# Seven half-block products for eight in the first product of the last MLP

## The chip, the cores and the metric

The kernel runs on one core of a Trainium2 chip. The metric is the device time of one execution in microseconds (us), lower is better; times given are the median of several executions. Engines are named as in the profile: PE is the matrix engine (TensorE), PEld its weight loads, DVE the vector engine, ACT the scalar engine, POOL GpSimd, SP the engine whose queue issues most of the transfers.

## The reference, cut to what matters

The network has two layers over 1024 tokens of width 1024. Each layer is a mixer and then an MLP with a squared ReLU of inner width 4096; a norm ends it. The change touches the MLP of the second layer.

```python
def sqrelu_mlp(h, w1, w2):
    return jnp.square(jax.nn.relu(h @ w1)) @ w2

def reference(x, ...):
    for layer in range(DEPTH):
        ...
        x = x + mix.astype(x.dtype)
        h = rmsnorm(x, norm_ffn_g[layer])
        x = x + sqrelu_mlp(h, mlp_w1[layer], mlp_w2[layer]).astype(x.dtype)
    return rmsnorm(x, final_norm_g)
```

## The kernel before, in words

The tokens are worked on as two halves of 512 (H). Activations lie transposed: 8 chunks (NK) of 128 features by 512 tokens. A product in float32 is made from three matmuls in the faster type fp32r: every operand is split into a rounded part and a rest, and `mm3` (L304 to L310) multiplies rounded weight by rounded input (L308), rounded weight by the input's rest (L309) and the weight's rest by the rounded input (L310). Each matmul has a weight tile of 128 by 128 and streams 512 columns.

`weights` (L275 to L300) brings weights in pieces of 256 KB: SP issues the transfer into `wraw` (L286), ACT casts it to `whi` (L291), and the rest `wlo` is a subtraction in `lo` (L266 to L272), two of three times on DVE and otherwise on POOL. `wraw`, `whi` and `wlo` are rings of 4 slots: a slot is written again when its last reader is done.

`mlp` (L1204) takes the inner width in 8 blocks of 4 tiles of 128 features (f-tiles). `first(fb, fts)` makes one f-tile after another: 8 chunks by 3 matmuls into one PSUM tile `mm` (a ring of 6), then ReLU and square on ACT (L1225, L1226), a cast to `hidh` (L1232) and the rest `hidl` (L272). `second(fb)` multiplies the block by its rows of the second weight matrix, 4 output pieces of 24 matmuls with two PSUM tiles each, and DVE adds each to the residual `x` (L1253). With `ahead` = 2, two f-tiles of block b+1 come before the second product of block b and two behind it. Both products of a block have 96 matmuls of 512 columns.

At the end of the program the last MLP runs first for the last block (7) of half 0, whose residual is `x0`. Then `final(0, x0)` (L1374) writes half 0's rows: for each of four groups u of 128 tokens it makes 4 transposes into the PSUM tile `lnn` and 4 into `lnl` (L1384), ACT squares and sums both (L1372), DVE adds the two sums (L1365), ACT takes a root (L1366), DVE a reciprocal (L1367) and two scaled copies into `fo` (L1390), and SP issues the transfer out (L1393). There is one `lnn` and one `lnl`, so the transposes of u+1 into a tile wait until DVE has copied u out of it. Then comes the last MLP for half 1, all 8 blocks, whose last block is closed by `final_rows` (L1397). A scheduler lays out each engine's order from the program, so that f-tiles of half 1's block 0 stand among the transposes of `final(0)`; within `second` and `first` PE's order is the order written.

Of the kernel before, what the change touches and what calls it, by code (L numbers as in the profile page):

```python
# [9 lines left out]
F32 = mybir.dt.float32  # L10
F32R = mybir.dt.float32r
AF = mybir.ActivationFunctionType
ALU = mybir.AluOpType
# [4 lines left out]
P = 128  # L18
D = 1024
S = 1024  # L20
H = 512
NK = D // P
# [23 lines left out]
class Net:  # L46
# [258 lines left out]
    def mm3(self, ps, whi, wlo, xhi, xlo, start, stop):  # L305
        mm = self.nc.tensor.matmul
        self.clk += 0.64
        mm(ps, lhsT=whi, rhs=xhi, start=start, stop=False)  # L308
        mm(ps, lhsT=whi, rhs=xlo, start=False, stop=False)  # L309
        return mm(ps, lhsT=wlo, rhs=xhi, start=False, stop=stop)  # L310

    def mmps(self):
        return self.mm.tile([P, H], F32, "mm")
# [191 lines left out]
    def norm0(self):  # L505
# [3 lines left out]
        self.r0 = yield from self.rstd(accs, self.eps[:, 0:1], self.tp)  # L509
        self.done.add("r0")  # L510

    def scaled(self, xs, r, gname, w):
        nc = self.nc
        his, los = self.hpair(w)
# [686 lines left out]
        return xs  # L1201


    def mlp(self, layer, halves, blocks, ahead, dve=None, close=None, keep=None, beside=None):  # L1204
# [7 lines left out]
        hids = {}  # L1212

        def first(fb, fts):
            hid = hids.setdefault(fb, [([], []) for _ in halves])
            for ft in fts:
                f = fb * 4 + ft
                whi, wlo = self.weight(w1[:, :, f * P:(f + 1) * P], NK, P, dve, (1, f), keep)
                for hh, (xs, (his, los)) in zip(hid, halves):
                    ps = self.mmps()  # L1220
                    for k in range(NK):
                        mm = self.mm3(ps, whi[k], wlo[k], his[k], los[k], k == 0, k == NK - 1)
                        yield 0
                    t = self.tp.tile([P, H], F32, name="rel", tag="rel")
                    nc.scalar.activation(out=t, in_=ps, func=AF.Relu)  # L1225
                    nc.scalar.activation(out=t, in_=t, func=AF.Square)  # L1226
                    hi = self.hid.tile([P, H], F32R, "hidh")
                    lo = self.hid.tile([P, H], F32R, "hidl")
                    if dve is False:
                        nc.scalar.copy(out=hi, in_=t)  # L1230
                    else:
                        nc.vector.tensor_copy(out=hi, in_=t)  # L1232
                    last = self.lo(lo, t, hi, True if beside else dve)
                    hh[0].append(hi)
                    hh[1].append(lo)
                    if beside:
                        beside(last, mm)

        def second(fb):
            hid = hids.pop(fb)  # L1240
            for oc in range(4):
                whi, wlo = self.weight(w2[:, fb * 4:fb * 4 + 4, oc * 256:(oc + 1) * 256], 4, 256, dve, (2, fb, oc), keep)
                for hh, (xs, _) in zip(hid, halves):
                    pss = [self.mmps() for _ in range(2)]
                    for ks in (range(3), range(3, 4)):
                        for o in range(2):
                            for k in ks:
                                mm = self.mm3(pss[o], whi[k][:, o * P:(o + 1) * P], wlo[k][:, o * P:(o + 1) * P], hh[0][k],
                                         hh[1][k], k == 0, k == 3)
                                yield 0  # L1250
                    for o in range(2):
                        x = xs[oc * 2 + o]
                        last = nc.vector.tensor_tensor(out=x, in0=pss[o], in1=x, op=ALU.add)  # L1253
                    if beside:
                        beside(last, mm)

        blocks = list(blocks)
        yield from first(blocks[0], range(4))
        for i, fb in enumerate(blocks):
            if i + 1 < len(blocks):  # L1260
                yield from first(blocks[i + 1], range(ahead))
            if close and i + 1 == len(blocks):
                (his, los), = hids.pop(fb)
# [185 lines left out]
    def run(self):  # L1449
        nc = self.nc  # L1450
# [6 lines left out]
        _, mp = self.pool("mm", bufs=1, space=PSUM)  # L1457
# [39 lines left out]
        def main():  # L1497
            yield from self.cols0(h0)
            h1 = yield from self.cols1()
            self.close(cmst)  # L1500
            yield "b"
            self.mm.slots = mmslots + [(self.sp, "sc1", 2)] * 2
            _, hidp = self.pool("hid", side="left")
            self.hslots = [(hidp, f"hid{i}") for i in range(8)]
            self.hid = Ring(self.hslots)
            _, self.tp = self.pool("tmp", bufs=3, side="left")
            self.nt, self.ntp = "rel", self.tp
            _, xp = self.pool("x0", side="left")
# [57 lines left out]
        self.conv_out(c1, x1)  # L1566
        n1 = self.norm(x1, "nf1", 1)
        self.go(self.mlp(1, [(x0, n0)], [7], 0))
        _, self.fp = self.pool("fin", bufs=1, side="right")
        gp = self.gfin = self.fp.tile([P, D], F32, name="gfin")  # L1570
        nc.scalar.dma_start(out=gp, in_=self.A["final_norm_g"].rearrange("(o d) -> o d", o=1).to_broadcast([P, D]))
        self.final(0, x0)
        self.go(self.mlp(1, [(x1, n1)], range(8), 2, close=lambda *a: self.final_rows(1, x1, *a)))
        while self.open:
            self.close()

# [28 lines left out]
```

## Time and profile before

| | |
|---|---|
| time, median of 3 executions | 2381.07 us (2380.44 to 2381.91) |
| profiled execution, its own time | 2379.74 us |
| its span | 2378.0 us |
| PE busy | 2308.1 us, 97% of the span |
| DVE, ACT, POOL busy | 1532.2, 1047.7, 542.8 us |
| mean granted PE clock (1 is full) | 0.992 |

Durations come from the profiled execution, which is 1.33 us under the median. The page's busy column counts a matmul from its start to the end that the profile models, and matmuls overlap; the pace of a stream of matmuls is read from the distance of their starts. "idle before <-" is idle time of the engine just before an instruction, and what ended it.

### The profile page before, as it was taken

How to read it: one execution, taken by the hardware profiler on the slowest of the kernel's cores; microseconds unless marked ns; L12 is line 12 of the kernel's file. 1: busy time of each engine (PE TensorE's matmuls, PEld its weight loads, DVE VectorE, ACT ScalarE, POOL GpSimd, SP SyncE). 2: the span in 40 equal slices, each digit the busy share in tenths (PEclk: the TensorE clock that was granted, in tenths of full speed). 3: DMA queues.
4: the chain of work that ended last, by engine and by line, in shares of the span. 5: the costliest groups of instructions: out<-in, count | busy, mean ns of one | idle time of the engine just before them, and what ended most of it. 6: DMA issues, size and time to landing. Idle time of an engine off the chain costs nothing.

```text
span 2378.0 us, 38508 instructions
## 1 busy us (share of the span) xinstructions
PE 2308.1 (97%) x14535; PEld 1856.4 (78%) x14535; DVE 1532.2 (64%) x2563; ACT 1047.7 (44%) x1874; POOL 542.8 (23%) x477
## 2 busy tenths in 40 slices
PE   8989889989999999999999999999999999999998
PEld 6767667767777787878888888888878778888887
DVE  7775743667555464569977653799999756533334
ACT  6546634556443332443443363534433544433333
POOL 2322433110111121322000000105555422221121
PEclk9999999999999999999999999999999999999999
DMA  7345234444445454546666665563323333433332
GB/s 219 111 110 153 83 88 132 109 127 123 136 143 178 126 175 133 169 133 200 198 195 191 194 183 172 144 188 98 98 89 98 99 93 94 129 95 98 98 97 85
DMA packets 417934, 320.12 MB, mean 135 GB/s; under 512 B 44642, under 2 KB 360276, under 8 KB 417748
## 3 DMA queue, kind: packets, MB, share of 16 engines
q1 hardware_dynamic: 413684, 309.79, 43.5%
q0 software_dynamic: 2176, 4.19, 0.6%
q10 hardware_dynamic: 1888, 3.67, 0.5%
q8 instruction: 114, 1.87, 0.3%
q14 instruction: 72, 0.59, 0.1%
HBM read 257.29 MB, written 60.29 MB: 134 GB/s over the span
## 4 chain that ended last, share of the span: by engine, by line
PE 75%; DVE 15%; DMA 4%; ACT 3%; issue 2%; SPq 0%; POOL 0%; DVEq 0%; ACTq 0%; POOLq 0%
PE mm L308 23%; PE mm L309 22%; PE mm L310 22%; DVE acc L1321 5%; DMA raw<-p 1%; PE sc L734 1%; DVE C L709 1%; DVE E L711 1%; PE sc L652 1%; DVE hidl L272 1%; PE sc L817 1%; PE sc L771 1%; DMA cx<-d 1%; DVE x L1253 1%; PE at L936 1%
## 5 line engine op out<-in xcount | busy, mean ns | idle before, releaser
L291 ACT CAST whi<-wraw 128x512 fp32r<-128x512 f32 x720 | 445.7, 621 | 986.9 <-PE mm L309 890.9
L308 PE MATMUL mm<-h,whi 128*128 128x512 f32 x1792 | 725.8, 406 | 7.1 <-ACT h L383 2.4
L310 PE MATMUL mm<-h,wlo 128*128 128x512 f32 x1792 | 704.1, 394 | 1.4 <-POOL wlo L272 1.4
L309 PE MATMUL mm<-h,whi 128*128 128x512 f32 x1792 | 703.3, 393 | 1.3 <-DVE h L272 1.0
L272 POOL TENSOR_TENSOR wlo<-wraw,whi 128x512 fp32r<-128x512 f32 x302 | 422.2, 1399 | 1233.8 <-ACT whi L291 1178.5
L1321 DVE SCALAR_TENSOR_TENSOR acc<-u,par,acc 128x512 f32<-128x512 f32 x480 | 429.8, 905 | 10.0
L308 PEld LDWEIGHTS mm<-h,whi 128*128 128x128 f32 x1792 | 339.7, 190 | 89.7 <-issue 12.8
L310 PEld LDWEIGHTS mm<-h,wlo 128*128 128x128 f32 x1792 | 339.1, 189 | 75.7 <-POOL wlo L272 2.3
L309 PEld LDWEIGHTS mm<-h,whi 128*128 128x128 f32 x1792 | 340.0, 190 | 69.0 <-issue 2.4
L308 PE MATMUL mm<-hidh,whi 128*128 128x512 f32 x992 | 389.4, 396 | 0.1
L309 PE MATMUL mm<-hidl,whi 128*128 128x512 f32 x992 | 386.0, 390 | 0.9 <-DVE hidl L272 0.9
L310 PE MATMUL mm<-hidh,wlo 128*128 128x512 f32 x992 | 384.5, 390 | 0.9 <-POOL wlo L272 0.9
L272 DVE TENSOR_TENSOR wlo<-wraw,whi 128x512 fp32r<-128x512 f32 x258 | 183.5, 712 | 200.9 <-ACT whi L291 193.2
L1253 DVE TENSOR_TENSOR x<-mm,x 128x512 f32<-128x512 f32 x248 | 166.5, 686 | 85.9 <-PE mm L310 85.5
L308 PEld LDWEIGHTS mm<-hidh,whi 128*128 128x128 f32 x992 | 186.2, 188 | 43.5 <-issue 4.2
L310 PEld LDWEIGHTS mm<-hidh,wlo 128*128 128x128 f32 x992 | 186.2, 188 | 40.3 <-POOL wlo L272 1.3
L309 PEld LDWEIGHTS mm<-hidl,whi 128*128 128x128 f32 x992 | 186.3, 188 | 40.0 <-DVE hidl L272 1.3
L272 DVE TENSOR_TENSOR hidl<-rel,hidh 128x512 fp32r<-128x512 f32 x109 | 84.9, 780 | 77.9 <-ACT hidh L1230 76.5
L1232 DVE CAST hidh<-rel 128x512 fp32r<-128x512 f32 x68 | 34.2, 506 | 89.8 <-ACT rel L1226 89.6
L1226 ACT ACTIVATE rel<-rel 128x512 f32<-128x512 f32 x128 | 80.6, 633 | 3.9 <-ACT rel L1225 0.4
L1225 ACT ACTIVATE rel<-mm 128x512 f32<-128x512 f32 x128 | 75.6, 593 | 2.2 <-DVE hidl L272 2.0
L1557 POOL COPY u<-u 128x30 f32<-128x30 f32 x8 | 3.2, 399 | 250.2 <-DVE acc L1321 250.2
(377 smaller groups left out, 2191.9 us busy)
## 6 DMA issues: line engine op xcount, KB each, us to landing
wraw<-in_mlp_w_dram SPq DMA_DIRECT2D x512, 256.0 KB
lo<-wlo SPq DMA_DIRECT2D x160, 256.0 KB
wlo<-lo SPq DMA_DIRECT2D x160, 256.0 KB
wraw<-in_cv_pw_w_dram SPq DMA_DIRECT2D x96, 256.0 KB
wraw<-in_hy_w_in_dram SPq DMA_DIRECT2D x80, 256.0 KB
wraw<-in_hy_w_out_dram SPq DMA_DIRECT2D x32, 256.0 KB
p<-stg SPq DMA_DIRECT2D x30, 256.0 KB
raw<-p SPq DMA_DIRECT2D x40, 128.0 KB
```

Of the source, the lines that this page charges most:

```text
L272: return eng.tensor_tensor(out=out, in0=x, in1=hi.bitcast(F32), op=ALU.subtract)
L291: nc.scalar.copy(out=hi, in_=raw)
L308: mm(ps, lhsT=whi, rhs=xhi, start=start, stop=False)
L309: mm(ps, lhsT=whi, rhs=xlo, start=False, stop=False)
L310: return mm(ps, lhsT=wlo, rhs=xhi, start=False, stop=stop)
L652: mm(ps[64 * q:64 * q + 64, u * P:(u + 1) * P], lhsT=src[hs, c * 64:(c + 1) * 64], rhs=ar[hs, :, c, :], start=(u == 0), stop=(u == 3), ski ...
L709: tt(out=j3[:, 0:n, 0:m], in0=a3[:, j, j + 1:16].unsqueeze(2).to_broadcast([64, n, m]), in1=x3[:, j:j + 1, 0:m].to_broadcast([64, n, m]), ...
L1225: nc.scalar.activation(out=t, in_=ps, func=AF.Relu)
L1226: nc.scalar.activation(out=t, in_=t, func=AF.Square)
L1232: nc.vector.tensor_copy(out=hi, in_=t)
L1253: last = nc.vector.tensor_tensor(out=x, in0=pss[o], in1=x, op=ALU.add)
L1321: nc.vector.scalar_tensor_tensor(out=acc, in0=u[:, j:j + H], scalar=self.pv(f"dw{j}", c), in1=acc, op0=ALU.mult, op1=ALU.add)
```

## The change

In the last MLP of half 1 the first product of blocks 1 to 7 goes over to `first_seven`. It takes f-tiles in pairs and the 1024 input features in two halves, so that the weight is a 2 by 2 arrangement of pieces A11, A12, A21, A22 (each 256 KB, four 128 by 128 tiles). DVE makes four sums of pieces, S1 to S4, and the 2 by 2 product is made of seven products of half the input's columns (256 tokens) in place of eight: 7 pieces by 4 tiles by 3 matmuls of 256 columns for a pair, that is 168 matmuls of 256 columns for a block in place of 96 of 512. Four accumulators r1 to r4 lie by twos in two PSUM tiles; ACT copies r1 (L1282 of the changed kernel), DVE combines the accumulators (L1284 to L1294), ACT applies ReLU, square and the cast.

`half_sums` makes the matching sums of half 1's input on DVE, rounds them on ACT and takes their rests. It is written behind block 7 of half 0 and before `final(0)`. Behind `final(0)` the pool of `x0` is closed, and a pool in its space adds 2, 3 and 3 slots to the rings `wraw`, `whi`, `wlo`.

```diff
+    def half_sums(self, xs, gname, w, v):
...
+        for c in range(NK // 2):
+            ys = []
+            for k in (c, c + NK // 2):
+                y = self.ntp.tile([P, H], F32, name="nt", tag=self.nt)
+                nc.vector.scalar_tensor_tensor(out=y, in0=xs[k], scalar=self.pv(gname, k), in1=self.r, op0=ALU.mult,
+                                               op1=ALU.mult)
+                ys.append(y)
+            ta, tb = (self.tp2.tile([P, H], F32, name="lt", tag="lt") for _ in range(2))
+            tt(out=ta[:, L], in0=ys[0][:, R], in1=ys[0][:, L], op=ALU.subtract)
+            tt(out=ta[:, R], in0=ys[1][:, R], in1=ta[:, L], op=ALU.subtract)
+            tt(out=tb[:, L], in0=ys[1][:, R], in1=ys[0][:, R], op=ALU.subtract)
+            tt(out=tb[:, R], in0=ys[1][:, L], in1=ta[:, R], op=ALU.subtract)
+            for n, t in enumerate((ta, tb)):
+                nc.scalar.copy(out=h[:, 0, 2 * c + n, :], in_=t)
+                self.lo(h[:, 1, 2 * c + n, :], t, h[:, 0, 2 * c + n, :])
...
+        def first_seven(fb, pairs):
...
+            for p in pairs:
+                A = {}
+                for i in range(2):
+                    f = fb * 4 + 2 * i + p
+                    for j in range(2):
+                        a = A[f"A{i + 1}{j + 1}"] = self.wraw.tile([P, 4, P], F32, "wraw")
+                        nc.sync.dma_start(out=a, in_=w1[:, 4 * j:4 * j + 4, f * P:(f + 1) * P])
+                for name, a, b, op in (("S1", "A21", "A22", ALU.add), ("S2", "S1", "A11", ALU.subtract),
+                                       ("S3", "A11", "A21", ALU.subtract), ("S4", "A12", "S2", ALU.subtract)):
+                    A[name] = self.mip.tile([P, H], F32, name="ws", tag="mi").rearrange("p (k f) -> p k f", k=4)
+                    tt(out=A[name], in0=A[a], in1=A[b], op=op)
+                ra, rb = self.mmps(), self.mmps()
+                r1, r2, r3, r4 = ra[:, L], ra[:, R], rb[:, L], rb[:, R]
...
+                    for a, b, r, begin in (("A11", "B11", r1, True), ("S2", "T2", r2, False), ("S3", "T3", r3, True),
+                                           ("S1", "T1", r4, False), ("A12", "B21", r1, False), ("A22", "T4", r3, False),
+                                           ("S4", "B22", r4, False)):
+                        whi = self.whi.tile([P, 4, P], F32R, "whi")
+                        nc.scalar.copy(out=whi, in_=A[a])
+                        wlo = self.wlo.tile([P, 4, P], F32R, "wlo")
+                        self.lo(wlo, A[a], whi)
+                        for c in range(4):
+                            self.mm3(r, whi[:, c, :], wlo[:, c, :], *self.seven[b](c), begin and c == 0, c == 3, True)
+                            yield 0
+                        if a == "A11":
+                            nc.scalar.copy(out=u2, in_=r1)
+                        elif a == "S2":
+                            tt(out=u2, in0=r2, in1=u2, op=ALU.add)
...
+                        else:
+                            tt(out=y1[:, R], in0=r4, in1=u2, op=ALU.add)
+                for k, y, raw in ((2 + p, y2, slice(0, H)), (p, y1, R)):
+                    nc.scalar.activation(out=y[:, raw], in_=y[:, raw], func=AF.Relu)
+                    nc.scalar.activation(out=y, in_=y, func=AF.Square)
...
         self.go(self.mlp(1, [(x0, n0)], [7], 0))
+        self.half_sums(x1, "nf1", 1, 0)
...
         self.final(0, x0)
-        self.go(self.mlp(1, [(x1, n1)], range(8), 2, close=lambda *a: self.final_rows(1, x1, *a)))
+        self.close(self.cmx0)
+        _, wp3 = self.pool("w3", side="left")
+        for ring, n, m in ((self.wraw, "wraw", 2), (self.whi, "whi", 3), (self.wlo, "wlo", 3)):
+            ring.slots = ring.slots + [(wp3, f"{n}{4 + i}") for i in range(m)]
+        self.go(self.mlp(1, [(x1, n1)], range(8), 2, seven=range(1, 8), close=lambda *a: self.final_rows(1, x1, *a)))
```

How the order on the engines moves, at three places. The first is PE at the end of half 0's last second product, where `final(0)`'s transposes (into `lnn` and `lnl`, L1384 before and L1476 after) meet block 0 of half 1. Before, the rows are these, and 30 matmuls of block 0 stand between the last transposes of one token group and the first of the next:

```order
L1384 MATMUL lnn<-ident,x_4739 128x128 x3
L308 MATMUL mm<-h,whi 128x512
L309 MATMUL mm<-h,whi 128x512
L310 MATMUL mm<-h,wlo 128x512
L308 MATMUL mm<-h,whi 128x512
L309 MATMUL mm<-h,whi 128x512
L1384 MATMUL lnl<-ident,x_4739 128x128
```

After the change the first group's transposes still stand among the 24 matmuls of one f-tile, whose last three are the first rows here; the other three groups then follow each other:

```order
L308 MATMUL mm<-h,whi 128x512
L309 MATMUL mm<-h,whi 128x512
L310 MATMUL mm<-h,wlo 128x512
L1476 MATMUL lnl<-ident,x_4739 128x128 x2
L1476 MATMUL lnn<-ident,x_4739 128x128 x4
L1476 MATMUL lnl<-ident,x_4739 128x128 x4
L1476 MATMUL lnn<-ident,x_4739 128x128 x4
L1476 MATMUL lnl<-ident,x_4739 128x128 x4
L1476 MATMUL lnn<-ident,x_4739 128x128 x4
L1476 MATMUL lnl<-ident,x_4739 128x128 x4
L308 MATMUL mm<-h,whi 128x512
```

The matmuls that stood between the groups have moved behind the last group.

The second place is DVE there. After the change the last two updates of `x0` (L1345) stand among `half_sums` (L524 to L531, and the rests `h`), and the first step of `final(0)` on DVE (L1457) stands behind the last of it:

```order
L1345 TENSOR_TENSOR x_4739<-mm,x_4739 128x512
L524 SCALAR_TENSOR_TENSOR nt<-x_10850,par,acc 128x512
L1345 TENSOR_TENSOR x_4739<-mm,x_4739 128x512
L524 SCALAR_TENSOR_TENSOR nt<-x_10850,par,acc 128x512
L272 TENSOR_TENSOR h<-lt,h 128x512
L528 TENSOR_TENSOR lt<-nt 128x256
L1264 TENSOR_TENSOR ws<-wraw 128x512
L530 TENSOR_TENSOR lt<-nt 128x256
L529 TENSOR_TENSOR lt<-nt,lt 128x256
L531 TENSOR_TENSOR lt<-nt,lt 128x256
L272 TENSOR_TENSOR wlo<-wraw,whi 128x512
L272 TENSOR_TENSOR h<-lt,h 128x512
L1457 TENSOR_REDUCE fss<-fss 128x1
```

All of these but the updates and the weight's rest are new before L1457.

The third place is a block in the steady part: on PE the end of piece A11 of one pair (into `mm_21604`), two matmuls of A11 of the next pair (`mm_21759`), and then piece S2 of the first pair, which goes to the other half of `mm_21604`:

```order
L308 MATMUL mm_21604<-h_10854,whi_21611 128x256
L309 MATMUL mm_21604<-h_10854,whi_21611 128x256
L310 MATMUL mm_21604<-h_10854,wlo_21613 128x256
L308 MATMUL mm_21759<-h_10854,whi_21766 128x256 [waits DVE_49,Activation_49]
L309 MATMUL mm_21759<-h_10854,whi_21766 128x256
L308 MATMUL mm_21604<-h_78,whi_21628 128x256 [waits Activation_49]
```

On ACT the cast of that next A11 (`whi_21766`, in the slot that `whi_21611` had) stands ahead of the copy of r1 out of `mm_21604`:

```order
L1275 CAST whi_21766<-wraw_21743 128x512 [waits DMAHW3_49,PE_49]
L1282 COPY su_21608<-mm_21604 128x256 [waits PE_49]
L1275 CAST whi_21783<-ws_21753 128x512 [waits DVE_49,PE_49,Pool_49]
```

Before, the place has 48 matmuls of 512 columns in a row, each f-tile in a PSUM tile of its own.

## Rows read from the trace of the kernel before

**Rows 1.** Waits of PE from 1990 us on: total us, times, longest.
```profile
PE lnn L308 <- ACT fo L1407: 0.2, 1, 0.2
```
**Rows 2.** Busy time by stretch of the last MLP, half 1.
```profile
core 0: us, PE busy (x) PEld busy (x) DVE busy (x) ACT busy (x) POOL busy (x), PEclk, DMA share, GB/s
1990.00:2005.00 15.00, 15.00 (x68) 12.43 (x67) 13.62 (x18) 6.81 (x13) 7.06 (x5) 1.00 0.29 86
2005.00:2050.00 45.00, 45.00 (x215) 37.16 (x214) 20.33 (x36) 18.98 (x43) 8.60 (x7) 1.00 0.43 135
2094.00:2137.00 43.00, 43.00 (x191) 35.60 (x190) 16.22 (x25) 14.48 (x24) 9.02 (x7) 1.00 0.33 98
```
**Rows 3.** Timeline of PE: first matmul of 96 in one stretch, and the first behind it.
```profile
2072.27 0.39 PE L308 MATMUL mm<-h,whi 128*128 128x512 f32 x1
...
2094.03 0.39 PE L308 MATMUL mm<-hidh,whi 128*128 128x512 f32 x1
```
**Rows 4.** Timeline of PE: 256-column matmuls of the attention with 128x128 weights.
```profile
123.81 0.28 PE L896 MATMUL at<-kl,q 128*128 128x256 f32 x1
...
124.16 1.02 PE L682 MATMUL sc<-krv,blk 128*128 128x512 f32 x2
```
**Rows 5.** Timeline of PEld: the weight load of the second of these.
```profile
123.81 0.19 PEld L894 LDWEIGHTS at<-kh,q 128*128 128x128 f32 x1
```
**Rows 6.** Groups by line: durations of kinds that the change adds (mean ns).
```profile
L792 DVE TENSOR_TENSOR F<-sc,F 128x256 f32<-128x256 f32 x16 | 6.7, 419 | 13.3 <-PE sc L790 13.3
L804 ACT COPY C<-sc 128x256 f32<-128x256 f32 x16 | 5.8, 371 | 30.0 <-PE sc L803 30.0
L291 ACT CAST whi<-wraw 128x512 fp32r<-128x512 f32 x134 | 83.2, 622 | 224.3 <-PE mm L309 220.2 <-PE lnl L310 3.3 <-issue 0.8
L1226 ACT ACTIVATE rel<-rel 128x512 f32<-128x512 f32 x33 | 20.6, 634 | 0.8
L1253 DVE TENSOR_TENSOR x<-mm,x 128x512 f32<-128x512 f32 x64 | 43.5, 691 | 33.3 <-PE mm L310 33.2
```
**Rows 7.** Timeline of PE: end of half 0's last product; transposes of group 1.
```profile
2013.94 0.39 PE L310 MATMUL mm<-hidh,wlo 128*128 128x512 f32 x1
...
2025.97 0.60 PE L1384 MATMUL lnn<-ident,x 128*128 128x128 f32 x4
2026.76 0.48 PE L308 MATMUL mm<-h,whi 128*128 128x512 f32 x1
```
**Rows 8.** Timeline of ACT behind the transposes of group 1.
```profile
2026.61 0.60 ACT L1372 ACTIVATE fj<-lnn 128x512 f32<-128x512 f32 x1
```
**Rows 9.** Timeline of DVE behind the transposes of group 1.
```profile
2028.69 0.75 DVE L1390 SCALAR_TENSOR_TENSOR fo<-lnn,fss,gfin 128x512 f32<-128x512 f32 x1
2029.36 0.74 DVE L1390 SCALAR_TENSOR_TENSOR fo<-lnl,fss,gfin 128x512 f32<-128x512 f32 x1
```
**Rows 10.** Timeline of DVE where the half's input is scaled, and of block 1.
```profile
2000.90 1.77 DVE L272 TENSOR_TENSOR wlo<-wraw,whi 128x512 fp32r<-128x512 f32 x1
2003.32 1.29 DVE L1253 TENSOR_TENSOR x<-mm,x 128x512 f32<-128x512 f32 x2 [0.65 <-PE mm L310]
...
2098.06 0.69 DVE L272 TENSOR_TENSOR wlo<-wraw,whi 128x512 fp32r<-128x512 f32 x1 [1.01 <-ACT whi L291]
```
**Rows 11.** Timeline of POOL in the same places.
```profile
2000.38 1.74 POOL L272 TENSOR_TENSOR h<-nt,h 128x512 fp32r<-128x512 f32 x1
...
2108.98 1.28 POOL L272 TENSOR_TENSOR wlo<-wraw,whi 128x512 fp32r<-128x512 f32 x1 [12.94 <-ACT whi L291]
```
**Rows 12.** Timeline of PE behind an idle stretch elsewhere, in half 0.
```profile
1753.92 0.47 PE L308 MATMUL mm<-h,whi 128*128 128x512 f32 x1 [1.89 <-DVE x L1253]
...
1754.51 0.63 PE L310 MATMUL mm<-h,wlo 128*128 128x512 f32 x1
...
1757.88 0.40 PE L309 MATMUL mm<-h,whi 128*128 128x512 f32 x1
```
**Rows 13.** The stretch after that idle time, columns as in rows 2.
```profile
1754.40:1757.80 3.40, 3.40 (x9) 2.64 (x9) 3.29 (x5) 0.00 (x0) 0.00 (x0) 0.50 0.26 77
```

More of the change, by code (lines that the diff above doesn't have):

```diff
@@ L303, in weight, with mm3 @@
         return self.weights([ap], a, b, dve, [key], keep)[0]
-    def mm3(self, ps, whi, wlo, xhi, xlo, start, stop):
+    def mm3(self, ps, whi, wlo, xhi, xlo, start, stop, shared=False):
         mm = self.nc.tensor.matmul
         self.clk += 0.64
-        mm(ps, lhsT=whi, rhs=xhi, start=start, stop=False)
-        mm(ps, lhsT=whi, rhs=xlo, start=False, stop=False)
-        return mm(ps, lhsT=wlo, rhs=xhi, start=False, stop=stop)
+        mm(ps, lhsT=whi, rhs=xhi, start=start, stop=False, skip_group_check=shared)
+        mm(ps, lhsT=whi, rhs=xlo, start=False, stop=False, skip_group_check=shared)
+        return mm(ps, lhsT=wlo, rhs=xhi, start=False, stop=stop, skip_group_check=shared)
     def mmps(self):
@@ L510, in norm0, with plain, summed @@
         self.done.add("r0")
+    def half_sums(self, xs, gname, w, v):
+        nc = self.nc
+        tt = nc.vector.tensor_tensor
+        his, los = self.hpair(w)
+        h = self.hp[v]
+        L, R = slice(0, H // 2), slice(H // 2, H)
+        for c in range(NK // 2):
[13 more added lines that the diff above has]
+                self.lo(h[:, 1, 2 * c + n, :], t, h[:, 0, 2 * c + n, :])
+        def plain(o, half):
+            return lambda c: (his[o + c][:, half], los[o + c][:, half])
+        def summed(q):
+            half = (L, R)[q % 2]
+            return lambda c: (h[:, 0, 2 * c + q // 2, half], h[:, 1, 2 * c + q // 2, half])
+        self.seven = dict(B11=plain(0, L), B21=plain(4, L), B22=plain(4, R), T1=summed(0), T2=summed(1), T3=summed(2),
+                          T4=summed(3))
     def scaled(self, xs, r, gname, w):
         nc = self.nc
+        self.r = r
         his, los = self.hpair(w)
@@ L1201, in w_out, with mlp @@
         return xs
-    def mlp(self, layer, halves, blocks, ahead, dve=None, close=None, keep=None, beside=None):
+    def mlp(self, layer, halves, blocks, ahead, dve=None, close=None, keep=None, beside=None, seven=()):
         nc = self.nc
@@ L1212, in mlp @@
         hids = {}
+        def first_seven(fb, pairs):
+            tt = nc.vector.tensor_tensor
+            hhi, hlo = hids.setdefault(fb, [([None] * 4, [None] * 4)])[0]
+            L, R = slice(0, H // 2), slice(H // 2, H)
+            for p in pairs:
[11 more added lines that the diff above has]
+                r1, r2, r3, r4 = ra[:, L], ra[:, R], rb[:, L], rb[:, R]
+                y1, y2 = (self.tp.tile([P, H], F32, name="rel", tag="rel") for _ in range(2))
+                su = self.mip.tile([P, H], F32, name="su", tag="mi")
+                u2, u3 = su[:, L], su[:, R]
+                with self.tc.manual_schedule(engines={mybir.EngineType.PE}):
+                    for a, b, r, begin in (("A11", "B11", r1, True), ("S2", "T2", r2, False), ("S3", "T3", r3, True),
[12 more added lines that the diff above has]
+                            tt(out=u2, in0=r2, in1=u2, op=ALU.add)
+                        elif a == "S3":
+                            tt(out=u3, in0=r3, in1=u2, op=ALU.add)
+                        elif a == "S1":
+                            tt(out=y2[:, R], in0=r4, in1=u3, op=ALU.add)
+                        elif a == "A12":
+                            nc.scalar.activation(out=y1[:, L], in_=r1, func=AF.Relu)
+                        elif a == "A22":
+                            tt(out=y2[:, L], in0=r3, in1=u2, op=ALU.add)
+                        else:
[3 more added lines that the diff above has]
+                    nc.scalar.activation(out=y, in_=y, func=AF.Square)
+                    hhi[k] = self.hid.tile([P, H], F32R, "hidh")
+                    hlo[k] = self.hid.tile([P, H], F32R, "hidl")
+                    nc.scalar.copy(out=hhi[k], in_=y)
+                    self.lo(hlo[k], y, hhi[k], True)
@@ L1214, in first @@
         def first(fb, fts):
+            if fb in seven:
+                yield from first_seven(fb, [f // 2 for f in fts if f % 2 == 0])
+                return
             hid = hids.setdefault(fb, [([], []) for _ in halves])
@@ L1507, in main @@
             self.nt, self.ntp = "rel", self.tp
-            _, xp = self.pool("x0", side="left")
+            self.cmx0, xp = self.pool("x0", side="left")
             x0 = xp.tile([P, NK, H], F32, name="x0")
```

## The prediction, on record before the change was run

> **What bounds the kernel now.** I first asked for PE's waits in the stretch that the change touches: from 1990 us to the end at 2378 us PE waits 0.2 us in all [rows 1]. The busy table by stretch says the same: PE fills every stretch at a granted clock of 1.00, while in a stretch of 43 us as long as a block DVE works 16.2, ACT 14.5 and POOL 9.0 us [rows 2]. So here the time is the number of matmuls times their pace: a matmul less is worth its pace, and a wait of PE costs its whole length, since nothing lies slack behind it. The pace is in the timeline: 96 matmuls of 512 columns lie between the starts 2072.27 and 2094.03 [rows 3], 21.76 / 96 = 0.2267 us each. (The 0.39 us in the rows is a duration with the overlapping end, not the pace.)
>
> DVE is the exception to "the other engines have room": while half 1's input is scaled, 1990 to 2005 us, it works 13.6 of 15 us [rows 2]. The change adds its input sums on DVE just there.
>
> **Part 1, the matmuls.** Seven blocks lose 7 x 96 = 672 matmuls of 512 columns: 672 x 0.2267 = 152.3 us. They gain 7 x 168 = 1176 of 256 columns. The trace has such matmuls with the same 128x128 weights in the attention: three of them lie between the starts 123.81 and 124.16 [rows 4], 0.117 us each. 1176 x 0.117 = 137.6 us. That is **-14.8 us**. The bounds: half of 0.2267 would give 1176 x 0.1133 = 133.3, -19.1 us; 0.120, with a few thousandths more on so short a stretch, gives -11.2 us. I take 0.117, which is the only row of this shape.
>
> A weight load takes 0.19 us [rows 5], longer than 0.117, and every matmul has one. In the row it starts at 123.81, with the matmul before its own, and it is not done when the matmul at 123.93 begins, which yet does not fall back to a pace of 0.19; so loads overlap one another and the matmuls, and I price them at nothing. The Trainium skill (TensorE: Matmul & The Clock Gate, Part 3: Packing small matmuls) says that a weight load overlaps matmuls in flight only when the row group differs. Here all weights use all row groups, so by that rule load and matmul would add up; the trace disagrees, with 0.117 us from start to start beside 0.19 us of load.
>
> **Part 2, DVE, ACT and POOL in the steady blocks.** A changed block needs on DVE 15 rests of weights and 4 of `hidl` (0.69 [rows 10]), 8 sums of pieces (0.69, same shape), 8 updates of x (0.691) and 10 combinations (0.419 [rows 6]): 18.6 + 5.5 + 4.2 = 28.3 us. POOL does 7 rests, 7 x 1.28 = 9.0 us [rows 11]. ACT does 22 casts (0.622), 8 square or ReLU steps of full width at 0.634, 4 casts to `hidh` and some half-wide steps at 0.371 [rows 6]: 22 us. The block on PE takes 168 x 0.117 + 96 x 0.2267 = 41.4 us, so PE's work covers all three, and I cost their sheer volume at nothing. The transfers are as many and as large as before and had 33% of the DMA engines [rows 2]; nothing too.
>
> What is not covered is in the order. Right behind piece A11 stand two matmuls of the next pair's A11, whose cast reuses the slot of `whi` that piece A11 still reads until its last matmuls; it can start only then. Behind it on ACT stands the copy of r1, and S2's first matmul waits for that copy because it goes to the same PSUM tile. So PE sees 0.62 + 0.37 [rows 6] and about 0.2 for the handing over, less the few matmuls between: about 1.1 us. This comes once in each of five steady periods, and about 1.5 us in the first changed block, whose pieces follow `final(0)` closely: **+7 us**. Bounds: 3 (cast early enough in half of the places) and 14 (twice that, if DVE is late too).
>
> **Part 3, the end of half 0.** This is the largest loss. Before, 30 matmuls lie between the transposes of one token group and the next, and they hide the chain between them: transposes at 2025.97 [rows 7], squares from 2026.61 [rows 8], the copy of `lnn` done at 2028.69 + 0.75 = 2029.44, of `lnl` at 2029.36 + 0.74 = 2030.10 [rows 9]. So `lnn` is free 3.47 us after a group began. A group occupies PE from 2025.97 to 2026.76, some 0.8 to 0.9 us. In the new order groups 1, 2 and 3 follow each other with nothing between, so between 1 and 2 and between 2 and 3 PE waits 3.47 - 0.87 = 2.6 us each: 5.2 us. Behind group 3 comes a tile of block 0 whose cast stands on ACT behind that group's squares: two squares and a cast after the transposes, less what overlaps, about 1.6 us.
>
> Before group 1 the wait depends on DVE. Between the start of the sums and the first step of `final(0)` DVE now has 8 scalings (0.75, as [rows 9]), 16 half-wide sums (0.419), 5 rests of sums, 5 of weights and one piece sum (0.69), 8 updates of `x0` (0.691): 6.0 + 6.7 + 7.6 + 5.5 = 25.8 us. It can begin at about 2000.9, where before a weight's rest began [rows 10]. So the first step of `final(0)` comes no sooner than 2026.7, and the two copies end about 2.2 us later; with 0.7 more for a collision with POOL (below) that is 2029.6. PE ends the last product at 2013.94 + 0.23 [rows 7], has the first group (0.87) and 24 matmuls (5.4 us) and could go on at 2020.6. It waits 9.0 us, partly already for the last updates of `x0`, which stand among the sums. Together 9.0 + 5.2 + 1.6 = **+15.5 us** rounded. Lower bound: no backlog, 2.6 in place of 9.0: 9.4. Upper bound: 20, with four more collisions. Loads of the new slots wait until group 3 is through; the 24 matmuls of the first tile behind (5.4 us) hide them, so nothing, though without that cover it would be about 2 us.
>
> **Part 4, the clock behind it.** PE's granted clock fell to 0.50, 1.2 GHz, for 3.4 us [rows 13] after PE had idled 1.89 us [rows 12]. In it 8 matmuls took 1754.51 to 1757.88, 0.42 us each in place of 0.2267: 1.6 us lost. Part 3 has three longer idle times, with little between them; I take **+2 us**, between 0 and 4.
>
> **Part 5, the end of the program.** The last block's last piece has a chain behind it: addition 0.42, ReLU 0.37, square 0.63, cast 0.62 [rows 6], in front of matmuls that need it, with three matmuls as cover: **+2 us** (0.5 to 3).
>
> **The sum.** -14.8 + 7 + 15.5 + 2 + 2 = +11.7 us. Against the profiled execution's own 2379.74 us (span 2378.0) that is 2391.4; that execution was 1.33 us under the median of the runs shown, so on the median's scale 2392.8, **2393 us**.
>
> **Rivals.** *The waits stay short (other side, faster).* The place is the end of half 0: if DVE fits the sums into its gaps and is not late, only the chain's 9.4 us are left; if also the steady stalls are at 3 and the pace is 0.1133, the sum is -19.1 + 9.4 + 3 + 0.5 = -6.2: 2375 us. It turns from slower to faster where all stalls together come to under 14.8 us, and is measurable under 10. For it: DVE works only 20.3 of 45 us from 2005 to 2050 [rows 2]. Against: what is new has to go before 2020, and DVE was full until 2005. Chance 0.16.
>
> *The stalls just eat the gain.* Stalls of 10 to 19 us in sum: 2376 to 2386 us, no change that can be told (0.2%, about 4.8 us, is what a measurement of this kernel can tell from none). Chance 0.14.
>
> *DVE and POOL bound the pairs.* A subtraction from two SBUF tiles took 1.77 us on DVE in place of 0.69 beside a POOL operation that ran from 2000.38 to 2002.12 [rows 10, 11]: it ended 0.55 us behind POOL's. If that meets some three of a block's seven POOL rests at a point where DVE is needed, a block loses 3 x 1.08 x three quarters, about 2.5 us: 7 x 2.5 = 17 more, 2410 us. The point from which it decides: 18.6 + 5.5 (the two-input work of DVE) + 9.0 + combinations 4.2 = 37.3 of the 41.4 us are taken if nothing of POOL's runs beside DVE. Against: 37.3 is still below 41.4. Chance 0.12. The Trainium skill (SBUF — State Buffer, Who interferes with whom) calls this an exclusive lock on a port pair, under which the later operation waits for the whole earlier one; the 0.55 us behind POOL's end agree with it.
>
> *The loads pace the short matmuls.* If loads did not overlap each other, the pace would be 0.19: 1176 x (0.19 - 0.117) = +86 us, 2479 us. Against: the starts, as said [rows 4, 5]. Chance 0.02. By the skill's rule above, load and matmul in turn, it would be 0.19 + 0.117 and still more.
>
> **How the numbers follow.** My own case, waits of 20 us or more in sum with DVE not the bound, has 0.56; with the two rivals that are slower 0.70 for slower by over 0.2%, 0.14 within 0.2%, 0.16 faster. The predicted time is that of my case, 2393. The low end takes in the "just eaten" case and most of the short-wait one down to 2376; the high end, 2408, is my case with the upper bounds of parts 2 and 3 not quite together (7 + 4.5 more), and the milder half of the DVE rival. My case alone is 2386 to 2404.
>
> **What would show it.** In the changed profile: PE's timeline behind 2014 should have idle times of some 9, 2.6 and 2.6 us before the transposes of groups 1 to 3, and the first full-width matmul behind group 3 near 2038; the granted clock should fall to 0.5 there. In a steady block 256-column matmuls should start 0.117 us apart, and the waits of PE should name ACT's cast and copy behind each A11. I am wrong in part 3 if the transposes of groups 1 to 3 start before 2025, in part 1 if the pace is over 0.125, and in part 2 if a steady period (168 short and 96 long matmuls) takes under 41.8 or over 44.5 us.

## The result and the profile after

The change made the kernel slower: 2408.18 us median of 4 executions (2404.05 to 2409.26) against 2380.76 us (2377.26 to 2381.91), ratio 1.0118, 95% interval 1.0104 to 1.0132. The sign was forecast, the size was not: 27 us in place of 12, 0.2 us over the range's upper end.

The profiled execution took 2409.26 us, span 2407.5. PE's waits from 1990 us on, which were 0.2 us in all before [rows 1] (what PE ran next, what it waited for, total, times, longest):

```profile
PE lnn L1476 <- DVE fo L1482: 8.0, 3, 3.1
PE mm L308 <- ACT whi L291: 5.3, 4, 2.6
PE mm L308 <- ACT whi L1275: 3.0, 5, 0.6
PE lnl L1476 <- DVE x L1345: 2.8, 1, 2.8
PE mm L310 <- DVE wlo L272: 2.3, 1, 2.3
PE lnn L308 <- ACT hidh L1300: 0.8, 1, 0.8
PE mm L308 <- DVE rel L1294: 0.5, 1, 0.5
```

These are 22.7 us. The table by stretch shows where, and that the clock fell with them (columns as in rows 2):

```profile
2005.00:2050.00 45.00, 29.57 (x108) 21.52 (x108) 30.61 (x58) 16.51 (x38) 10.18 (x7) 0.76 0.29 96
2094.00:2137.00 43.00, 40.42 (x239) 36.50 (x238) 27.28 (x45) 20.32 (x37) 9.80 (x7) 0.92 0.33 100
2137.00:2180.00 43.00, 42.41 (x265) 38.03 (x264) 27.29 (x44) 20.25 (x38) 9.90 (x7) 1.00 0.32 97
...
2023.00:2028.00 5.00, 5.00 (x12) 3.94 (x13) 4.99 (x10) 1.19 (x2) 0.00 (x0) 0.50 0.36 105
2034.00:2045.50 11.50, 5.32 (x24) 3.98 (x24) 4.17 (x10) 5.24 (x16) 0.07 (x1) 0.54 0.35 138
2045.50:2052.00 6.50, 6.34 (x14) 4.55 (x15) 4.85 (x8) 1.41 (x3) 1.28 (x1) 0.50 0.82 264
```

Between 2005 and 2050 us PE works 29.6 of 45 us at a mean granted clock of 0.76, where it was 45.0 at 1.00 [rows 2]. PE's timeline there:

```profile
2019.45 0.33 PE L1476 MATMUL lnl<-ident,x 128*128 128x128 f32 x1 [2.80 <-DVE x L1345]
...
2022.99 0.79 PE L310 MATMUL mm<-h,wlo 128*128 128x512 f32 x1 [2.28 <-DVE wlo L272]
2023.58 0.63 PE L308 MATMUL mm<-h,whi 128*128 128x512 f32 x1
...
2030.53 0.38 PE L1476 MATMUL lnl<-ident,x 128*128 128x128 f32 x2
2034.05 0.63 PE L1476 MATMUL lnn<-ident,x 128*128 128x128 f32 x4 [3.14 <-DVE fo L1482]
...
2037.84 1.12 PE L1476 MATMUL lnn<-ident,x 128*128 128x128 f32 x4 [2.41 <-DVE fo L1482]
...
2042.21 1.12 PE L1476 MATMUL lnn<-ident,x 128*128 128x128 f32 x4 [2.40 <-DVE fo L1482]
...
2045.53 0.80 PE L308 MATMUL mm<-h,whi 128*128 128x512 f32 x1 [1.34 <-ACT whi L291]
```

The three groups stand where the forecast put their waits, but group 1 begins at 2034.05, not 2029.6, the distances are 3.79 and 4.37 us, not 3.47 (at half clock the transposes themselves take twice as long: 1.12 against 0.60 [rows 7]), and the first full-width matmul comes at 2045.5, not 2038. Why group 1 is late shows in the row at 2030.53, on ACT and on DVE:

```profile
2030.50 0.62 ACT L1275 CAST whi<-wraw 128x512 fp32r<-128x512 f32 x1 [2.45 <-PE mm L309]
2031.02 0.61 ACT L533 CAST h<-lt 128x512 fp32r<-128x512 f32 x1
2031.54 0.59 ACT L1464 ACTIVATE fj<-lnl 128x512 f32<-128x512 f32 x1
```
```profile
2031.15 0.69 DVE L272 TENSOR_TENSOR wlo<-wraw,whi 128x512 fp32r<-128x512 f32 x1 [2.69 <-ACT whi L1275]
...
2032.36 0.15 DVE L1457 TENSOR_REDUCE fss<-fss 128x1 f32<-128x2 f32 x1
```

The last two transposes of group 0 stand behind the f-tile's 24 matmuls. Just before these PE had waited for an update of `x0` (2.80 us) and among them for a weight's rest (2.28 us), and twelve of them ran at half clock, so PE came to the two transposes only at 2030.53. From there the rest of group 0's chain takes 3.52 us to group 1's start, about the 3.47 us that the forecast read for a whole group. ACT's queue adds some 0.6 us to it: the square of group 0 stands behind two casts, the first of which waits for a `whi` slot that PE frees only at the end of the f-tile. DVE had its half-wide sums done by 2028.5 and then idled 2.69 us for that cast; it was not DVE's volume alone.

From the gaps between starts in the trace I worked out where each microsecond over the pace went (before: 1.1 us in the whole stretch). Predicted terms beside it, in us:

| part | predicted | measured |
|---|---|---|
| matmuls, 1176 short for 672 long | -14.8 | -11.8 (pace 0.1195) |
| end of half 0 with its clock (to 2060 us) | 15.5 + 2 | 25.1 |
| first changed blocks, to 2115 us | 1.5 | 6.6 (2.5 of it at half clock) |
| five steady periods | 5.5 | 4.4 |
| 512-column matmuls slower than 0.2267 | none | 3.5 |
| end of the program | 2 | 1.5 |
| sum | 11.7 | 29.3 |

The profiled executions differ by 29.5 us.

### The profile page after: what moved, and what is told of

It reads as the page before. It is cut to its first block, busy times and chain, and to the rows that moved or that the text cites. A ratio compares the mean times of both kernels' runs of the same rounds, so it can differ in the third digit from the quotient of the medians.

```text
span 2407.5 us, 39912 instructions
## 1 busy us (share of the span) xinstructions
PE 2319.5 (96%) x15039; PEld 1882.2 (78%) x15039; DVE 1631.1 (68%) x2731; ACT 1097.9 (46%) x1980; POOL 553.3 (23%) x481
## 5 line engine op out<-in xcount | busy, mean ns | idle before, releaser
L291 ACT CAST whi<-wraw 128x512 fp32r<-128x512 f32 x664 | 410.6, 620 | 825.5 <-PE mm L309 715.9
L308 PE MATMUL mm<-h,whi 128*128 128x512 f32 (+1 forms) x1960 | 754.5, 386 | 11.1 <-ACT whi L1275 3.0
L310 PE MATMUL mm<-h,wlo 128*128 128x512 f32 (+1 forms) x1960 | 729.3, 374 | 3.8 <-DVE wlo L272 2.3
L309 PE MATMUL mm<-h,whi 128*128 128x512 f32 (+1 forms) x1960 | 730.0, 373 | 1.3 <-DVE h L272 1.0
L272 POOL TENSOR_TENSOR wlo<-wraw,whi 128x512 fp32r<-128x512 f32 x290 | 407.8, 1407 | 1129.6 <-ACT whi L291 990.1
L308 PEld LDWEIGHTS mm<-h,whi 128*128 128x128 f32 x1960 | 374.7, 191 | 88.2 <-issue 12.0
L310 PEld LDWEIGHTS mm<-h,wlo 128*128 128x128 f32 x1960 | 373.6, 191 | 71.7 <-POOL wlo L272 3.1
L309 PEld LDWEIGHTS mm<-h,whi 128*128 128x128 f32 x1960 | 375.5, 192 | 62.9 <-issue 2.4
L1345 DVE TENSOR_TENSOR x<-mm,x 128x512 f32<-128x512 f32 x248 | 165.9, 685 | 57.7 <-PE mm L310 57.5
L272 DVE TENSOR_TENSOR hidl<-rel,hidh 128x512 fp32r<-128x512 f32 x117 | 95.1, 813 | 97.4 <-ACT hidh L1322 76.5
L1318 ACT ACTIVATE rel<-rel 128x512 f32<-128x512 f32 x100 | 63.0, 632 | 3.2 <-ACT rel L1317 0.4
L1275 ACT CAST whi<-ws 128x512 fp32r<-128x512 f32 x56 | 34.6, 619 | 63.8 <-PE mm L309 55.5
L272 POOL TENSOR_TENSOR wlo<-ws,whi 128x512 fp32r<-128x512 f32 x21 | 29.8, 1417 | 129.9 <-ACT whi L1275 100.8
```

The source lines that it names most:

```text
L272: return eng.tensor_tensor(out=out, in0=x, in1=hi.bitcast(F32), op=ALU.subtract)
L291: nc.scalar.copy(out=hi, in_=raw)
L308: mm(ps, lhsT=whi, rhs=xhi, start=start, stop=False, skip_group_check=shared)
L309: mm(ps, lhsT=whi, rhs=xlo, start=False, stop=False, skip_group_check=shared)
L310: return mm(ps, lhsT=wlo, rhs=xhi, start=False, stop=stop, skip_group_check=shared)
L1275: nc.scalar.copy(out=whi, in_=A[a])
```

## The experiments

The part of the program ahead of half 0's last second product has the same work in all kernels, yet that product's first matmul falls anywhere from 1987.9 to 1995.8 us. So beside each ratio I give the **stretch** from this matmul to the program's last one, read from the profiled execution: 378.6 us before, 408.0 after. It is one execution of each kernel, and its distance from the kernel before differs from what the ratio says by up to 5.5 us; a difference of 2 or 3 us between two stretches is an indication and no proof.

**Sums alone.** The changed kernel with `seven=range(1, 8)` taken out of the last call, the pool `w3` and the ring lines too.

> The kernel before plus the input sums alone (half_sums behind block 7 of half 0), with all blocks' first products as before and no new slots. Theory A (the new slots in x0's space force the transposes of half 0's last norm into one group, and that group is the larger part of the 22 us lost there; the sums only make DVE late): the transposes stay apart, PE waits 5 to 9 us for DVE, 2386 to 2390 us. Theory B (the sums on DVE are the cause, the slots cost nothing): PE loses some 20 us there, 2399 to 2403 us.

Ratio 1.0015 (1.0006 to 1.0025), stretch 381.8, +3.2 us; the median of 2381.9 is under what theory A expected. Theory B's 20 us are not there. DVE works 31.8 of 45 us there, but 30 matmuls stand between the transposes, and PE waits little:

```profile
PE mm L309 <- DVE hidl L272: 1.0, 1, 1.0
PE mm L308 <- ACT whi L291: 0.6, 1, 0.6
```

**New slots alone.** `seven=` and `half_sums` taken out, the slots kept.

> The kernel before plus the new slots alone (x0's pool closed behind the final norm of half 0, rings of 6, 7 and 7 slots), no sums, all first products as before. Theory A: the transposes of groups 1 to 3 stand together, three waits of about 2.6 us and one of 1.6 us, and the clock falls to 0.5 behind them (3 to 5 us): 2392 to 2396 us. Theory B: within 2 us of before, 2379 to 2383 us.

Ratio 1.0091 (1.0071 to 1.0111), median 2399.9, over theory A's range; stretch 395.8, +17.2 us: some 12 of it in the end of half 0, 5.5 in something not foreseen (below). The transposes stand together, with no sums at all:

```profile
2023.37 0.66 PE L1476 MATMUL lnn<-ident,x 128*128 128x128 f32 x4 [1.20 <-DVE fo L1482]
...
2027.09 1.11 PE L1476 MATMUL lnn<-ident,x 128*128 128x128 f32 x4 [2.40 <-DVE fo L1482]
...
2031.46 1.11 PE L1476 MATMUL lnn<-ident,x 128*128 128x128 f32 x4 [2.41 <-DVE fo L1482]
```

So the grouping comes from the slots: `whi` tiles of block 0 lie in x0's space, so their f-tiles cannot go ahead of x0's last transposes. Theory B falls.

**Rings lengthened later.** In `mlp`, behind the first product of block 0:

```diff
         yield from first(blocks[0], range(4))
+        if grow:
+            grow()
```

where `grow` holds the three ring lines; then the same behind `first(blocks[i + 1], range(ahead))` for i = 0, one pair later.

> The changed kernel with the rings lengthened only behind the first product of block 0 of half 1, so that block 0 uses the old slots. Theory A: group 1 and group 2 stand apart again, groups 2 and 3 still together: 10 to 14 us less than the changed kernel's 2408, that is 2394 to 2398 us. Theory B: no more than 3 us less, 2405 to 2408 us.

> The changed kernel with the rings lengthened only behind the first changed pair (block 1's first), the sums where the change puts them. All three later groups of transposes stand apart again. Theory A (grouping by the slots is some 20 of the 27 us): 2380 to 2386 us. Theory C (the seven-product blocks themselves lose as much, through waits for casts and late loads): 2390 us or more.

First place: ratio 1.0060 (1.0045 to 1.0075), stretch 392.8, median 2394.0, as theory A expected. Second place: 1.0044 (1.0029 to 1.0059), stretch 385.9, 22.1 us less than after (by the ratios 17.6), though the median of 2387.8 is 2 us over what theory A expected. The transposes stand apart (2034.60, 2043.56 and 2049.86 us), and no wait on their PSUM tiles is left; the first pair still waits:

```profile
2046.88 0.38 PE L308 MATMUL mm<-h,whi 128*128 128x256 f32 x1 [1.20 <-ACT su L1282]
...
2056.22 0.70 PE L308 MATMUL mm<-hidh,whi 128*128 128x512 f32 x2 [2.45 <-DVE hidh L1324]
2059.69 0.50 PE L310 MATMUL mm<-hidh,wlo 128*128 128x512 f32 x1 [1.00 <-DVE wlo L272]
```

Behind the pause of 2.45 us the granted clock stayed at 1.00 (2056 to 2060 us).

**No new slots.** The ring lines are taken out, all else as the change has it.

> The changed kernel without any new slots, rings of 4, so the transposes stand apart, but a changed pair has only 4 slots for its 7 cast pieces and 4 raw pieces. Theory A with slots that are worth little: 2380 to 2386 us. If the added slots are needed for the pace of the steady blocks: more waits of PE for casts in every block, 2 us or more in each of seven, 2394 us or more.

Ratio 1.0111 (1.0096 to 1.0126), stretch 404.9. In the steady blocks PE waits again and again, for copies, casts and combinations, so the larger rings are needed:

```profile
PE mm L308 <- ACT su L1282: 2.7, 3, 0.9
PE mm L308 <- ACT hidh L1300: 2.4, 2, 1.2
```

(Waits from 2150 to 2280 us.) What had to change was when the rings grow, not that they do.

**Sums later: two attempts that do not separate them.** First the call of `half_sums` moved behind `final(0, x0)`.

> The changed kernel with the input sums made behind the final norm of half 0 in place of ahead of it. Theory A: the transposes still stand together, only DVE's lateness goes (waits ahead of group 1 from about 10 to about 3 us): 2398 to 2402 us. Theory B: almost all of the loss at half 0's end goes, 2386 to 2390 us.

Ratio 1.0110 (1.0089 to 1.0131), stretch 403.3. The scheduler gave DVE the same place for the sums as before, since they are ready there whatever the program's order; this run tests nothing. Then a real dependence: the call behind the new pool, and the scaled inputs in x0's space:

```diff
-                y = self.ntp.tile([P, H], F32, name="nt", tag=self.nt)
+                y = self.wp3.tile([P, H], F32, name="nt", tag=f"wraw{4 + k // 4}", bufs=1)
```

> The changed kernel with the scaled inputs of the sums written into slots in x0's space, so that the sums cannot start before half 0's last transposes; the new slots stay as the change has them, so the transposes still stand together. If DVE's lateness through the sums costs what the changed kernel's trace puts down to DVE ahead of group 1 (waits of 2.8, 2.3 and most of 3.1 us and a clock fall of 2.3 us): 8 to 10 us less than the changed kernel, 2398 to 2400 us. If the sums cost only the 3.4 us that they cost alone, with spread transposes: 2403 to 2406 us.

Ratio 1.0133 (1.0112 to 1.0153), median 2410.7, over both expectations; stretch 409.9. The waits for an update and for a rest ahead of group 1 are gone, and one wait of 13.84 us has come, for a cast whose raw load landed only then; the kernel gives its slots to the sums first:

```profile
2051.91 0.80 PE L308 MATMUL mm<-h,whi 128*128 128x512 f32 x1 [13.84 <-ACT whi L291]
```

What the sums cost beside grouped transposes is known only by difference: up to 2060 us the changed kernel lost 25.1 us and the run with the slots alone some 12, so about 13 us go to the sums together with the first pair's casts and piece sums, which stand there too. Alone the sums cost 3.2.

**The short matmuls' pace.** The kernel before, each 512-column matmul of the first products of blocks 1 to 7 in two halves.

> The kernel before with each 512-column matmul of the first product of blocks 1 to 7 cut into two of 256 columns, eight half products with no sums: 7 x 192 matmuls of 256 columns for 7 x 96 of 512. If the short matmuls' pace is 0.117 us as in the attention: +4.9 us; if it is 0.1217 as the steady blocks of the changed kernel show: 7 x 192 x 0.1217 - 152.3 = +11.2 us, 2389 to 2393 us, and the starts in its timeline lie 0.12 apart. If the larger pace comes from the seven-product form only (more weights per column), it stays near 2385.

Ratio 1.0047 (1.0032 to 1.0062), stretch 387.7, +9.0 us. Twenty-one starts in a row, first and last:

```profile
2165.52 0.28 PE L308 MATMUL mm<-h,whi 128*128 128x256 f32 x1
...
2167.91 0.28 PE L310 MATMUL mm<-h,wlo 128*128 128x256 f32 x1
```

2.39 / 20 = 0.1195, and 1344 x 0.1199 (the mean of all of them) - 152.3 = +8.8. The pace belongs to the shape, not to the seven-product form.

**Eight slots of `whi`, six of `wlo`,** lengthened behind the first pair.

> As the changed kernel with the rings lengthened behind the first changed pair, but whi with 8 slots and wlo with 6. If the wait in each steady period (0.87 us from start to start behind piece A11) is for the whi slot that A11 holds, it shrinks to under 0.3 us in all five periods and the time falls by 2 to 3 us against the run with 7 slots; if it is for the copy out of the PSUM tile, it stays.

Ratio 1.0035 (1.0024 to 1.0045), stretch 388.0 against 385.9, so no gain of 2 to 3 us. The distance behind A11 falls from 0.87 to 0.50 us, not under 0.3, and a wait of 0.6 us for POOL's rest comes for it, with one `wlo` slot fewer. So the wait was partly the slot; what was left is the next experiments' question.

**Five blocks, sums late.** Seven products in blocks 2 to 6 alone; sums in x0's space, made behind block 1's first two f-tiles, where `whi` grows by 4 and `wlo` by 3; then also the pieces' rests on DVE (`self.lo(wlo, A[a], whi, True)`).

> Seven products in blocks 2 to 6 alone; rings lengthened behind block 1's first two f-tiles, whi by 4 and wlo by 3; sums in x0's space as in the run before. Gain by the measured pace 0.1195 us: 5 x (21.76 - 168 x 0.1195) = 8.4 us; lost: about 1 us in each of 4 or 5 steady periods and 1 to 2 us around the first changed pair, no loss at half 0's end and none at the program's end. Theory A: 1 to 4 us under the kernel before. Theory C (the sums or the pairs bring waits wherever they stand): at or over it.

> As the run with blocks 2 to 6, but the rests of the changed pieces all on DVE, none on POOL. If the waits for POOL's rest (0.7 us in each steady period with 8 slots) are POOL's length, they go: 2 to 3 us less than that run, 3 to 6 us under the kernel before. If DVE with some 32 of 41 us a block is then late itself, no gain.

Ratios 1.0050 (1.0033 to 1.0067) and 1.0046 (1.0029 to 1.0063), stretches 389.1 and 389.6: no gain in either. PE waits 5.7 us once for an update of x behind the late sums and then runs at half clock. Making the sums late costs more than making them early: the second of the two differs from the run with new space below in this alone, 389.6 against 386.4. Theory C holds for this place.

**Where the weights lie.** All of x0's space to `wraw`, the old `wraw` slots to `whi` and `wlo`, otherwise as the run with the rings lengthened behind the first pair:

```diff
+            old = self.wraw.slots
+            self.whi.slots, self.wlo.slots = self.whi.slots + old[0:2], self.wlo.slots + old[2:4]
+            self.wraw.slots = [(wp3, f"wraw{4 + i}") for i in range(8)]
```

> As the changed kernel with the rings lengthened behind the first changed pair, but all of x0's space goes to wraw (8 slots there), and whi and wlo get the 4 old wraw slots (6 slots each), so that no weight that PE reads lies in x0's space. In all runs with new slots the 512-column matmuls behind them start 0.230 to 0.232 us apart in the mean, in all runs without them 0.2267 to 0.2274. If it is where the weights lie that PE reads: back to 0.227 here, some 3 us less by that alone. If it is the transfers or the busier engines: it stays at 0.231. Waits for casts may grow, with one slot fewer.

Mean pace of the 512-column matmuls from 2140 to 2220 us: 0.2277 us here, 0.2316 with the weights in x0's space. Ratio 1.0061 (1.0048 to 1.0075), stretch 391.6: six slots bring new waits, as allowed for, that outweigh it. In the run with the slots alone the two paces stand side by side, 43 distances and then 34:

```profile
2204.24 0.39 PE L308 MATMUL mm<-hidh,whi 128*128 128x512 f32 x1
...
2214.27 0.40 PE L309 MATMUL mm<-hidl,whi 128*128 128x512 f32 x1
...
2216.11 0.39 PE L308 MATMUL mm<-hidh,whi 128*128 128x512 f32 x1
...
2223.82 0.39 PE L309 MATMUL mm<-h,whi 128*128 128x512 f32 x1
```

10.03 / 43 = 0.2333 and 7.71 / 34 = 0.2268. In the same run's first products the slow distances begin at the first matmul of a piece (2089.5 us) and go on for 36 matmuls, the three pieces in the new slots of a ring of 7, and for some eight more.

**Five blocks, sums early, both placings of the weights.**

> Seven products in blocks 2 to 6, sums early as the change has them, slots as in the run before this one, rests of the pieces on DVE. Gain 5 x (21.76 - 168 x 0.1195) = 8.4 us; lost: 3.2 for the sums, about 0.5 to 1 in each steady period, 1 to 2 around the first pair. From the start of half 0's last second product to the last matmul (378.6 us before): 375 to 379 us, so at most 3 us under the kernel before; a time clearly under it would need the waits to be gone too.

> As the run before this one, with whi and wlo lengthened in x0's space (8 and 7 slots) in place of the exchange. If weights in x0's space cost 0.004 us for each 512-column matmul: some 3 us more than that run, unless the larger rings save as much in waits.

Old space: ratio 1.0033 (1.0020 to 1.0045), stretch 381.4, over the 375 to 379 expected. New space: 1.0056 (1.0044 to 1.0069), stretch 386.4, 5.0 more. What is left in the first is one wait per period, for the copy:

```profile
2161.89 0.28 PE L310 MATMUL mm<-h,wlo 128*128 128x256 f32 x1
2163.03 0.38 PE L308 MATMUL mm<-h,whi 128*128 128x256 f32 x1 [0.87 <-ACT su L1282]
```

**A tile of its own.** The run with the old space, with r2 in a third PSUM tile, where S2 begins its own sum:

```diff
-                ra, rb = self.mmps(), self.mmps()
-                r1, r2, r3, r4 = ra[:, L], ra[:, R], rb[:, L], rb[:, R]
+                ra, rb, rc = self.mmps(), self.mmps(), self.mmps()
+                r1, r2, r3, r4 = ra[:, L], rc[:, R], rb[:, L], rb[:, R]
```

> As the run with blocks 2 to 6 and the weights in the old space, but accumulator r2 in a PSUM tile of its own, so that piece S2 no longer waits for ACT's copy of r1 out of the same tile. If that shared tile is the wait of 1.0 us (1.14 from start to start) behind piece A11 in each of six places: the waits on the copy go, 5 to 6 us less in the stretch from half 0's last second product to the last matmul (381.4 us there, 378.6 before), so 375 to 377 us and some 2 us under the kernel before, too little to tell in the total time. If the third PSUM tile of a pair runs the ring of 6 dry, new waits for DVE's updates take their place and it stays at 380 or more.

Ratio 1.0005 (0.9995 to 1.0016), stretch 376.7: 4.7 us less, 1.9 us under the kernel before. The copy's waits are gone:

```profile
PE mm L310 <- DVE wlo L272: 1.4, 4, 0.3
PE mm L308 <- ACT whi L291: 1.0, 2, 0.6
PE mm L308 <- ACT rel L1318: 0.9, 1, 0.9
PE mm L308 <- DVE x L1345: 0.2, 1, 0.2
```

In their place come four waits of up to 0.3 us for a rest on DVE. So both links that the forecast named are in the wait behind A11: more slots shorten it to 0.50 us, a tile of its own ends the wait for the copy. This is the best version found, and its total time cannot be told from that of the kernel before; none beats it clearly.

## Why the prediction was right in sign and wrong in size

The forecast was 11.7 us and the trace shows 29.3. The miss of 17.6 us is 7.6 at the end of half 0, 5.1 in the first changed blocks, 3.5 in the 512-column matmuls and 3.0 in the short matmuls' pace, less 1.6 where the forecast was too high.

**Part 1, matmuls: right mechanism, gain too large by 3 us.** The pace came from three distances of a short stretch, 0.117; the form's own is 0.1195, inside the bounds that were given. Loads cost nothing more, as forecast: 0.12 us from start to start beside loads of 0.19. The Trainium skill (TensorE: Matmul & The Clock Gate, Part 3: Packing small matmuls) says that a weight load overlaps matmuls in flight only when the row group differs. The 1344 short matmuls of the run with halves, each with its own load of a 128x128 weight, do not agree with it.

**Part 2, steady blocks: right; first changed blocks: too small.** From start to start 0.87 us behind A11 in five periods, where the pace is 0.12, and 4.4 us in all against 5.5:

```profile
2148.05 0.28 PE L310 MATMUL mm<-h,wlo 128*128 128x256 f32 x1
2148.92 0.39 PE L308 MATMUL mm<-h,whi 128*128 128x256 f32 x1 [0.59 <-ACT whi L1275]
```

The volume is covered, as said: DVE 27.3, ACT 20.3 and POOL 9.9 of 43 us, PE 42.4. The first changed blocks were undersized, 6.6 for 1.5: a raw load that landed late held DVE's piece sums, these the casts on ACT, and PE waited 2.6 us until 2107 us, with half clock behind it:

```profile
2102.97 0.69 DVE L1264 TENSOR_TENSOR ws<-wraw 128x512 f32<-128x512 f32 x1 [2.45 <-DMA wraw<-in_mlp_w_dram]
```
```profile
2105.56 1.20 ACT L1275 CAST whi<-ws 128x512 fp32r<-128x512 f32 x2 [4.69 <-DVE ws L1264]
```
```profile
2107.34 0.80 PE L308 MATMUL mm<-hidh,whi 128*128 128x512 f32 x1 [2.58 <-ACT whi L291]
```

**Part 3, the end of half 0: place and order right, the waits near their size.** With part 4 the sum was 17.5 against 25.1 measured. (The three terms 9.0, 5.2 and 1.6 add up to 15.8, not to the 15.5 set down.) From the starts, the wait before group 1 comes to 9.0 us for 9.0, the time between the groups to 6.4 for 5.2 and that behind group 3 to 2.5 for 1.6; waits of some 1.3 us before 2010 had not been priced. The 9.0 is luck in part: the forecast had group 0's chain run behind DVE's backlog, and it came after PE's own delay, as the row at 2030.53 shows. The distance of the groups, 3.47 us, was read at full clock.

The forecast also gave the sums the largest share of the loss there, the 9.0 us. They have such a price only beside grouped transposes. The sums alone cost 3.2 us, the slots alone some 12 us there, and with the transposes spread but the sums in place only 3.6 us (of the 25.1) are left up to 2053 us. Which part of the change brings the transposes together, the new slots, the forecast had not asked.

**Part 4, the clock: the step that failed.** It took one fall of 3.4 us behind one pause of 1.89 us as its measure: 2 us. But several pauses follow each other here, and the granted clock stood at 0.50 from 2023 to 2028, at 0.54 from 2034 to 2045.5 and at 0.50 again to 2052. The 27 matmuls of block 0 that ran in it took 12.1 us in place of 6.1 (0.5 us of that are short waits), 5.9 us for 2 and over the upper bound of 4, and the slower transposes come on top. The wait at 2107 was followed by half clock too, 2.5 us that had no term. Together that is some 6 us of the 17.6, more than any other step; the late raw load of part 2, the slower 512-column matmuls and the pace follow with about 3 us each.

**Not in the forecast at all:** the slower 512-column matmuls, 3.5 us. There was no term for the place of the new slots.

**Rivals.** "The waits stay short" named its place correctly: the sign hangs on the end of half 0. All stalls together came to 41 us, where its point was 14.8, so it is out, and "the stalls just eat the gain" with it. DVE and POOL as the bound are out by the volumes above, and loads that pace the short matmuls by the pace. None of the three signs of being wrong that the forecast gave came (the pace 0.1195, a steady period of 43.2 us, the groups behind 2025): none of them asked how long the clock would stay low.

## What to carry to other kernels

Where a pool's space is handed on, ask who must be finished before the first tile in it can be written, and what stood between that work in the queue: here a ring that grew one block too early pulled filler matmuls out from between dependent transposes and cost more than the arithmetic saved. A wait on a path with cover and one without are priced differently, so two added loads must be priced together, not each against the old trace. And a pause of a full engine can be paid again behind it, by the clock: a train of pauses kept it at half for most of 2034 to 2052 us, where a single pause of 2.45 us in the run with late rings left it at 1.00. So price the whole train and not one fall.

## What the runs showed of the hardware that was not expected

512-column matmuls whose weights lie in the space that x0 had start 0.2333 us apart, those with weights in the old slots 0.2268 (one run, alternating); the mean is 0.2267 to 0.2274 in the four runs without new slots and 0.230 to 0.232 in all with weights in the new ones, and is 0.2274 to 0.2277 in the three runs that put only raw loads there. It is shown that the place of weights read by PE sets it; why that place is slower stays open. The mean of the 256-column matmuls does not show it: 0.1186 to 0.1195 with the new slots, 0.1196 to 0.1200 without.
